# A streaming encoder layer on one core: all transposes of a PSUM bank issued before their reads, reads on two engines, norm and weight steps spaced anew, and down-projection loads one feature tile further on

## The chip, the cores and the metric

One Trainium2 chip, and one of its cores. The metric is the device time of one execution in microseconds; lower is better. The instructions of the core run on TensorE (PE in the profile, its weight loads PEld), VectorE (DVE), ScalarE (ACT), GpSimd (POOL) and SyncE (SP). In this kernel every DMA is issued by SP, in one queue.

## The reference

One layer of a streaming encoder for 1024 prompt positions and 8 samples of 16 positions (1152 rows of 1024 features, float32), both with the same weights. Cut to what matters here:

```python
def run_layer(x, c, ...):
    sh1, sc1, gt1, sh2, sc2, gt2 = ada_params(c, w_ada, b_ada)
    h = modulate(rms_norm(x, norm1_g), sh1, sc1)
    q, k, v, ub, vb, g_a, g_b = mixer_inputs(h, w_in, ...)
    ...                                   # band attention o_a, spatial gating o_b
    mixed = (g_a * (o_a @ w_out_a) + g_b * (o_b @ w_out_b)) @ w_out
    x = x + gt1 * mixed
    h2 = modulate(rms_norm(x, norm2_g), sh2, sc2)      # h * (1 + scale) + shift
    f, conv_state = conv_ffn(h2, conv_cache, ...)
    x = x + gt2 * f
    ...

def conv_ffn(h, conv_cache, w_ffn_in, ffn_conv_w, ffn_conv_b, w_ffn_out):
    g, u = jnp.split(h @ w_ffn_in, 2, axis=-1)         # 2816 features each
    gp = jnp.concatenate([conv_cache, g], axis=1)
    gc = ffn_conv_b
    for j in range(3):
        gc = gc + ffn_conv_w[j] * gp[:, j:j + T]
    return (jax.nn.gelu(gc) * u) @ w_ffn_out, gp[:, -2:]
```

## The kernel before, in words

The rows are nine tiles of 128 (tiles 0 to 7 the prompt, tile 8, called `NTP`, the samples). Every float32 product is done as three passes over a high and a low part: `split` (L76) copies the high part on ACT and subtracts on DVE for the low part. `load_w` (L80) is a DMA into a staging tile (`wst`, five buffers) and a split into a weight tile (`wp`, nine buffers).

The change lies in the second half of the kernel, which has three parts.

**Output projection and norm (L1124 to L1169).** Three passes: half 0 of the columns for tiles 8, 0, 1, 2, 3; half 1 for all nine; half 0 for 4 to 7. A tile and a half of the columns are eight steps k, and one step is three matmuls (`mxps`, L1140). After the eight steps DVE multiplies by the gate (L1153) and the old rows are added (L1154; on POOL in passes 0 and 1, on DVE in pass 2). When both halves of a tile are there, SP stores it (L1159), ACT squares it (L1116), POOL makes the factor (L125, L126), and DVE scales the tile in place (L1111). `later` holds these steps with the step number at which they enter the queues. The weights of the next pass are split during the last tile of a pass, one per step. PE, ACT and DVE run here in the order in which the program is written (`by_hand`, L1080); SP and POOL are ordered by the scheduler.

`between` writes, between the steps, the work for the first half of the feed-forward's rows: it transposes the scaled rows on PE into a bank of PSUM (`h2ps`, two banks), and `modulated` (L917) reads them with scale and shift into SBUF. Its items carry a tile, a flag and costs for ACT and DVE; `fill_in` emits one when the tile is far enough and both `credit` counters are above zero. `block_pair_1` does the same for the second half of the rows: eight items for tiles 3, 4, 5 (L999 to L1002), tile 6, two splits (`A11`, `A12`), tile 7, then sums and splits. For tiles 6 and 7 it writes one transpose, then its read, then the next transpose into the same bank, four times for each bank.

**Up-projection (L1354 to L1373).** 22 feature tiles f, two units u each (the halves of the rows). A unit is seven products X, Y, Z of 12 matmuls (L1199) with seven weight combinations B11, B21, T2, T1, T3, T4, B22 (`up_weights`, L1040), then the convolution, the GELU and a store to `aT_d`. The order by hand goes on until f = 0 is done, and the remaining items of `block_pair_1` are written into f = 0. Before f = 0 the convolution cache is loaded (`ccr`, L1184) and transposed (`ccps`, L1187). From f = 1 on, the scheduler orders all engines.

**Down-projection (`down_steps`, L1304).** Three groups of three row tiles; each goes over the 22 feature tiles, with three `load_w` for each f (`a`, `wfo_0`, `wfo_1`) and 18 matmuls (`fops`, L1320). The steps of f = 0 of the first group are written into the last feature tile of the up-projection. After it stand `conv_rows` (PE transposes, a DVE copy and five stores) and the loads of the last gate (`gate_rows`, 18 DMAs). At the end of a group, f = 20 and 21 are done accumulator by accumulator, and each is multiplied, added to the rows and stored (L1349 to L1351).

Of the kernel before, what the change touches and what calls it, by code (L numbers as in the profile page):

```python
# [12 lines left out]
ALU = mybir.AluOpType  # L13
AX = mybir.AxisListType

P = 128
D = 1024
KD = D // P
# [20 lines left out]
def tile_layer(ctx: ExitStack, tc: tile.TileContext, io):  # L39
# [30 lines left out]
    def tpps(name, n=512):  # L70
        return banks["pool"].tile([P, 512], F32, tag="tp", name=name, bufs=banks["tp"])[:, :n]
# [110 lines left out]
    r = 0  # L182
# [770 lines left out]

    ORDER = [NTP] + list(range(NTP))

    def between():


        o = opnd[0]
        yield 1, True, 0.65, 0.7  # L960
        o.raws(RAWS[:2])
        for h in range(2):
            ps = tpps(f"h2psS_{h}")
            for i in range(4):
                pe.transpose(ps[:, i * P:(i + 1) * P], x1[NTP][:, (4 * h + i) * P:(4 * h + i + 1) * P], ident)
            o.modulated_samples(RAWS[h], h, ps, 0)
            yield 1, True, 0.0, 1.4
        for k in range(KD):
            o.modulated(RAWS[k // 4], k, x1_T((0, 1), k, "0")[:, 0:QB - P], P)
            yield 1, True, 0.45, 0.0  # L970
        o.raws(RAWS[2:])
        yield 2, False, 1.3, 1.4
        o.chunks(0, ("A11h", "A11l", "A12h", "A12l", "A22h"))
        for n in ("A11", "A12"):
            o.split(n, HOME[n])
            yield 3, True, 1.3, 1.4
        for k in range(KD):
            o.modulated(RAWS[2 + k // 4], k, x1_T((1, 2, 3), k, "1")[:, 32:32 + QB], 0)
            yield 3, True, 0.65, 0.0
        o.raws(["S1"])  # L980
        for n in ("S1", "S3", "S2", "S4"):
            sums(o, (n,))
            yield 3, True, 0.0, 1.4
        for n in ("S2", "S1"):
            o.slots((n + "h", n + "l"))
            o.split(n, HOME[n])
            yield 3, True, 1.3, 1.4
        yield 5, False, 1.3, 1.4
        o.chunks(1, ("S3h", "S3l", "A22l", "S4h", "S4l"))
        for n in ("S3", "A22", "S4"):  # L990
            o.split(n, HOME[n])
            yield 5, False, 1.3, 1.4

    def block_pair_1():

        o = opnd[1]
        o.raws(RAWS)
        for k in range(KD):
            ps = x1_T((3, 4, 5), k, "2")  # L999
            o.modulated(RAWS[k // 4], k, ps[:, 64:64 + QB], 0)  # L1000
            o.modulated(RAWS[2 + k // 4], k, ps[:, 64 + QB:], 0)
            yield  # L1002
        for t in (6, 7):
            if t == 7:
                for n in ("A11", "A12"):
                    o.slots((n + "h", n + "l"))
                    o.split(n, HOME[n])
                    yield
            for h in range(2):
                ps = tpps(f"h2ps{t}_{h}")  # L1010
                for i in range(4):
                    pe.transpose(ps[:, i * P:(i + 1) * P], x1[t][:, (4 * h + i) * P:(4 * h + i + 1) * P], ident)
                    o.modulated(RAWS[2 + h], 4 * h + i, ps[:, i * P:(i + 1) * P], 32 + P * (t - 6))
            yield
        o.raws(["S1"])
        sums(o, ("S1", "S3", "S2"))
        o.chunks(2, ("A22h", "A22l", "S1h", "S3h", "S2h"))
        low_slot(o, "S2")
        yield
        sums(o, ("S4",))  # L1020
        low_slot(o, "S1")
        yield
        low_slot(o, "S3")
        yield
        o.split("A22", "22")
        yield
        o.slots(["S4h"])
        low_slot(o, "S4")
        yield
# [78 lines left out]

    def scale_tile(t, ss):
        r = rstd_of(ss, 1, D, nrm, f"x1n{t}r")  # L1110
        later.append((step_n + 3, lambda: dve.tensor_scalar(x1[t], x1[t], r, None, ALU.mult)))  # L1111
        scaled_at[t] = step_n + 5

    def square_tile(t):
        ss = nrm.tile([P, 1], F32, tag="ss", name=f"x1n{t}ss", bufs=4)
# [13 lines left out]
    for i, (blk, tiles) in enumerate(passes):  # L1129
        for t in tiles:  # L1130
# [6 lines left out]
            for k in range(KD):  # L1137
                w = wos[i][k]
                for n, (a, b) in enumerate(((hi, 0), (hi, 1), (lo, 0))):
                    pe.matmul(ps, lhsT=a[:, k, o:o + P], rhs=w[:, b, :], start=(k == n == 0), stop=(k == KD - 1 and n == 2))  # L1140
                step_n += 1
                for e in credit:
                    credit[e] = min(credit[e] + 0.72, 2.0)
                if t == tiles[-1] and next(loads[i + 1], loads) is not loads:
                    spend(0.63, 0.69)
                do_later()
                item = fill_in(item)
                if i == 2 and t == tiles[-1]:
# [5 lines left out]
            (pool if i < 2 else dve).tensor_tensor(x1[t][:, bs], x1[t][:, bs], xr, ALU.add)  # L1154
            spend(0.0, 0.7 if i < 2 else 1.4)
# [148 lines left out]
    def down_steps():  # L1304
        for g in range(3):
# [14 lines left out]
                    pe.matmul(acc[t, hf], lhsT=a[:, x, o], rhs=w[hf][:, y, :], start=(f == 0 and i == 0), stop=(f == NF - 1 and i == 2))  # L1320

            weights(0)
            for f in range(NF - 2):
                if f:
                    weights(f)
                for t in ts:
                    for hf in range(2):
                        step(f, t, hf)
                        if g == 0 and f == 0:
                            yield  # L1330
                if g == 0 and f == 0:
                    conv_rows()
                    g2p, g2s = stile(D, "g2p"), stile(D, "g2s")
                    for j in range(2):
# [1 line left out]

            for f in (NF - 2, NF - 1):
                weights(f)
            for t in ts:
                xr = stile(D, f"x1r{t}")  # L1340
                sp.dma_start(xr, x1_d[t * P:(t + 1) * P, :])
                y = stile(D, f"y{t}")
                gt = g2p if t < NTP else g2s
                dst = io["o_yp"].rearrange("b s d -> (b s) d")[t * P:(t + 1) * P, :] if t < NTP else io["o_ys"].rearrange("b s d -> (b s) d")
                for hf in range(2):
                    for f in (NF - 2, NF - 1):
                        step(f, t, hf)
                    hs = slice(512 * hf, 512 * (hf + 1))
                    dve.tensor_tensor(y[:, hs], acc[t, hf], gt[:, hs], ALU.mult)  # L1349
                    dve.tensor_tensor(y[:, hs], y[:, hs], xr[:, hs], ALU.add)  # L1350
                    sp.dma_start(dst[:, hs], y[:, hs])  # L1351
# [54 lines left out]
```

## Time and profile before

| | us |
|---|---|
| median of 3 runs | 1714.07 (1711.29 to 1717.16) |
| the profiled execution | 1715.13 |
| its span | 1713.3 |
| PE busy | 1654.2 |
| DVE busy | 917.8 |
| ACT busy | 731.4 |
| POOL busy | 338.2 |

PE is busy for 97% of the span. The page cuts the span into 40 slices of 42.8 us; each digit is the busy share in tenths, and a row of its own gives the TensorE clock that was granted. A matmul that runs at a lower clock counts as busy all the same, so both rows have to be read together.

### The profile page before, as it was taken

How to read it: one execution, taken by the hardware profiler on the slowest of the kernel's cores; microseconds unless marked ns; L12 is line 12 of the kernel's file. 1: busy time of each engine (PE TensorE's matmuls, PEld its weight loads, DVE VectorE, ACT ScalarE, POOL GpSimd, SP SyncE). 2: the span in 40 equal slices, each digit the busy share in tenths (PEclk: the TensorE clock that was granted, in tenths of full speed). 3: DMA queues.
4: the chain of work that ended last, by engine and by line, in shares of the span. 5: the costliest groups of instructions: out<-in, count | busy, mean ns of one | idle time of the engine just before them, and what ended most of it. 6: DMA issues, size and time to landing. Idle time of an engine off the chain costs nothing.

```text
span 1713.3 us, 28803 instructions
## 1 busy us (share of the span) xinstructions
PE 1654.2 (97%) x10788; PEld 1502.1 (88%) x10788; DVE 917.8 (54%) x1972; ACT 731.4 (43%) x1592; POOL 338.2 (20%) x506
## 2 busy tenths in 40 slices
PE   6999999999999999999887899999999998999998
PEld 5798888799998989998775899999999997888887
DVE  4552111137657543464365777776777664455554
ACT  5442111135655544552346444544444543334342
POOL 5410000024224200043222222222222210000000
PEclk9999999999999999999997999999999999999999
DMA  9125434421100132384321222222222224566664
GB/s 356 60 71 164 153 132 138 164 69 34 51 27 23 38 111 99 105 265 137 128 92 54 83 78 77 69 74 74 70 68 74 78 82 151 180 227 199 215 213 163
DMA packets 165552, 198.88 MB, mean 116 GB/s; under 512 B 14120, under 2 KB 124180, under 8 KB 165413
## 3 DMA queue, kind: packets, MB, share of 16 engines
q1 hardware_dynamic: 165413, 197.04, 35.8%
q8 instruction: 85, 1.39, 0.3%
q14 instruction: 54, 0.44, 0.1%
HBM read 161.48 MB, written 37.57 MB: 116 GB/s over the span
## 4 chain that ended last, share of the span: by engine, by line
PE 82%; DVE 5%; DMA 3%; ACT 3%; issue 3%; POOL 1%; SPq 1%; DVEq 0%; ACTq 0%; POOLq 0%
PE X L1199 15%; PE fops L1320 15%; PE Z L1199 8%; PE Y L1199 4%; PE o L688 2%; PE gbps L103 2%; PE qkps L101 2%; PE gbps L101 2%; PE gbps L102 2%; PE qkps L103 2%; PE qkps L102 2%; PE gaps L101 2%; PE gaps L102 2%; PE gaps L103 2%; PE adaps L382 2%
## 5 line engine op out<-in xcount | busy, mean ns | idle before, releaser
L1320 PE MATMUL fops<-wfo,a 128*128 128x512 f32 x1188 | 273.5, 392 | 6.6 <-ACT wfo L77 6.3
L1320 PEld LDWEIGHTS fops<-wfo,a 128*128 128x128 f32 x1188 | 224.5, 189 | 54.0 <-ACT wfo L77 6.7
L1199 PE MATMUL X<-op,wT 128*128 128x288 f32 x1144 | 194.8, 297 | 1.4 <-ACT u L1267 1.3
L1199 PEld LDWEIGHTS X<-op,wT 128*128 128x128 f32 x1144 | 169.1, 190 | 2.4 <-ACT u L1267 2.3
L1140 PE MATMUL mxps<-wo,mT 128*128 128x512 f32 x432 | 105.4, 399 | 2.9 <-ACT wo L77 1.8
L1140 PEld LDWEIGHTS mxps<-wo,mT 128*128 128x128 f32 x432 | 80.7, 191 | 20.4 <-ACT wo L77 2.5
L1232 DVE SCALAR_TENSOR_TENSOR gc<-gp,parT,gc 128x288 f32<-128x288 f32 (+2 forms) x110 | 67.6, 630 | 44.8 <-ACT gc L1231 44.8
L101 PE MATMUL qkps<-wqk,h1T 128*128 128x256 f32 x288 | 83.5, 290 | 0.8 <-ACT qf L582 0.8
L102 PE MATMUL qkps<-wqk,h1T 128*128 128x256 f32 x288 | 81.9, 284 | 0.0
L103 PE MATMUL qkps<-wqk,h1T 128*128 128x256 f32 x288 | 81.8, 284 | 0.0
L1231 ACT ACTIVATE gc<-gp,parT 128x288 f32<-128x288 f32 (+2 forms) x110 | 58.8, 572 | 39.1 <-DVE gp L1218 29.1
L1234 ACT ACTIVATE gc<-gc 128x288 f32<-128x288 f32 x88 | 39.0, 443 | 72.0 <-DVE gc L1233 72.0
L1059 POOL TENSOR_TENSOR t<-b,b 128x512 f32<-128x512 f32 x22 | 29.2, 1328 | 195.5 <-DVE wB L78 161.3
L101 PE MATMUL gaps<-h1T,wga 128*128 128x384 f32 x192 | 66.6, 347 | 0.0
L103 PE MATMUL gbps<-h1T,wgb 128*128 128x384 f32 x192 | 65.9, 343 | 0.0
L102 PE MATMUL gaps<-h1T,wga 128*128 128x384 f32 x192 | 65.0, 339 | 0.0
L101 PE MATMUL gbps<-h1T,wgb 128*128 128x384 f32 x192 | 64.9, 338 | 0.0
L102 PE MATMUL gbps<-h1T,wgb 128*128 128x384 f32 x192 | 64.7, 337 | 0.0
L78 DVE TENSOR_TENSOR wB<-b,wB 128x512 fp32r<-128x512 f32 x66 | 57.1, 867 | 13.5 <-ACT wB L77 12.2
L103 PE MATMUL gaps<-h1T,wga 128*128 128x384 f32 x192 | 64.2, 338 | 0.0
L1269 DVE TENSOR_TENSOR upb<-Z,u 128x288 f32<-128x288 f32 x44 | 20.0, 454 | 79.5 <-ACT u L1267 79.5
L78 DVE TENSOR_TENSOR wfo<-wfo_0s,wfo 128x512 fp32r<-128x512 f32 x66 | 45.7, 693 | 24.8 <-ACT wfo L77 24.6
(488 smaller groups left out, 4423.1 us busy)
## 6 DMA issues: line engine op xcount, KB each, us to landing
adaw<-in_w_ada_dram SPq DMA_DIRECT2D x48, 512.0 KB, 5.3
b<-in_w_ffn_in_dram SPq DMA_DIRECT2D x88, 256.0 KB, 4.0
wfo_0s<-in_w_ffn_out_dram SPq DMA_DIRECT2D x66, 256.0 KB, 3.0
wfo_1s<-in_w_ffn_out_dram SPq DMA_DIRECT2D x66, 256.0 KB, 2.6
aT_d<-gc SPq DMA_DIRECT2D x88, 144.0 KB, 2.8
mb_d<-sgb SPq DMA_DIRECT2D x8, 576.0 KB, 3.4
ga_d<-ga SPq DMA_DIRECT2D x24, 192.0 KB, 1.8
sga<-ga_d SPq DMA_DIRECT2D x8, 576.0 KB, 4.9
```

Source lines behind the costliest of these rows:

```text
L78: (eng or dve).tensor_tensor(lo, src, hi.bitcast(F32), ALU.subtract)
L101: pe.matmul(ps, lhsT=ah, rhs=bh, start=(i == 0), stop=False)
L102: pe.matmul(ps, lhsT=ah, rhs=bl, start=False, stop=False)
L103: pe.matmul(ps, lhsT=al, rhs=bh, start=False, stop=(i == n - 1))
L382: pe.matmul(ps[32 * j:32 * j + 32, :], lhsT=cT[:, k, :], rhs=st[j // 2][:, (j % 2) * 512:(j % 2 + 1) * 512], start=(k == 0), stop=(k == KD ...
L688: pe.matmul(o[hs, :], lhsT=v[:, k0 // P + i, hs], rhs=out[t, x][:, i * P:(i + 1) * P], start=(i == 0), stop=(i == nk - 1))
L1140: pe.matmul(ps, lhsT=a[:, k, o:o + P], rhs=w[:, b, :], start=(k == n == 0), stop=(k == KD - 1 and n == 2))
L1199: pe.matmul(ps, lhsT=w[:, wj, ks], rhs=x, start=(begin and n == 0), stop=(n == 11), skip_group_check=True)
L1231: act.activation(g, a0, AF.Identity, bias=bb, scale=w0)
L1232: dve.scalar_tensor_tensor(g, a1, w1, g, ALU.mult, ALU.add)
L1234: act.activation(gc, gc, AF.Gelu_apprx_tanh)
L1320: pe.matmul(acc[t, hf], lhsT=a[:, x, o], rhs=w[hf][:, y, :], start=(f == 0 and i == 0), stop=(f == NF - 1 and i == 2))
```

## The change

- A helper `transposed(t, h)` writes the four transposes of a bank and returns the bank. Tile 8 uses it (same order as before); for tiles 6 and 7 the four transposes of a bank now stand ahead of their four reads, and the reads go to ACT and DVE in turn.
- For tiles 3, 4, 5 the two reads of a bank go to ACT for even k and to DVE for odd k (all on ACT before).
- In `block_pair_1` the split of A11 follows tile 6, and that of A12 follows tile 7.
- A tile's square enters 3 steps after its store (2 before), the scaling 4 steps after the factor (3 before), and its transposes may follow 7 steps after the factor (5 before).
- The weights of the next pass begin one step earlier (the last step of the tile before the last). In pass 2 only four of the seven weight combinations of f = 0 are split; the other three (T3, T4, B22) are split in the first three steps of f = 0. `between` emits nothing in the last tile of pass 1.
- The old rows are added on POOL in pass 0 alone, on DVE in passes 1 and 2.
- After the passes no item of `block_pair_1` is written any more; tile 6 follows the first product of f = 0, the scaling of tile 7 stands after the second product's convolution, and tile 7's transposes follow the third product.
- `down_steps` asks for the loads of f + 1 ahead of the steps of f; `conv_rows` and the gate loads stand after f = 3 (f = 0 before). PE's order at the end of each group is fixed as written, and the last half row of the last tile is multiplied, added and stored in two halves.

```diff
+    def transposed(t, h):
+        ps = tpps(f"h2psT{t}_{h}")
+        for i in range(4):
+            pe.transpose(ps[:, i * P:(i + 1) * P], x1[t][:, (4 * h + i) * P:(4 * h + i + 1) * P], ident)
+        return ps
...
-            o.modulated(RAWS[k // 4], k, ps[:, 64:64 + QB], 0)
-            o.modulated(RAWS[2 + k // 4], k, ps[:, 64 + QB:], 0)
+            o.modulated(RAWS[k // 4], k, ps[:, 64:64 + QB], 0, k % 2 == 0)
+            o.modulated(RAWS[2 + k // 4], k, ps[:, 64 + QB:], 0, k % 2 == 0)
             yield
-        for t in (6, 7):
+        for t, n in ((6, "A11"), (7, "A12")):
+            for h in range(2):
+                ps = transposed(t, h)
+                for i in range(4):
+                    o.modulated(RAWS[2 + h], 4 * h + i, ps[:, i * P:(i + 1) * P], 32 + P * (t - 6), i % 2 == 0)
             if t == 7:
-                for n in ("A11", "A12"):
-                    o.slots((n + "h", n + "l"))
-                    o.split(n, HOME[n])
-                    yield
-            for h in range(2):
-                ps = tpps(f"h2ps{t}_{h}")
-                for i in range(4):
-                    pe.transpose(ps[:, i * P:(i + 1) * P], x1[t][:, ...], ident)
-                    o.modulated(RAWS[2 + h], 4 * h + i, ps[:, i * P:(i + 1) * P], 32 + P * (t - 6))
+                yield
+            o.slots((n + "h", n + "l"))
+            o.split(n, HOME[n])
             yield
...
-        later.append((step_n + 3, lambda: dve.tensor_scalar(x1[t], x1[t], r, None, ALU.mult)))
-        scaled_at[t] = step_n + 5
+        later.append((step_n + 4, lambda: dve.tensor_scalar(x1[t], x1[t], r, None, ALU.mult)))
+        scaled_at[t] = step_n + 7
...
-                if t == tiles[-1] and next(loads[i + 1], loads) is not loads:
-                    spend(0.63, 0.69)
+                last = t == tiles[-1]
+                if (last and (i < 2 or k in (1, 3, 5))) or (t == tiles[-2] and k == KD - 1):
+                    if next(loads[i + 1], loads) is not loads:
+                        spend(0.63, 0.69)
                 do_later()
-                item = fill_in(item)
+                if i != 1 or not last:
+                    item = fill_in(item)
...
-            (pool if i < 2 else dve).tensor_tensor(x1[t][:, bs], x1[t][:, bs], xr, ALU.add)
+            (pool if i == 0 else dve).tensor_tensor(x1[t][:, bs], x1[t][:, bs], xr, ALU.add)
...
-                later.append((step_n + 2, lambda t=t: square_tile(t)))
-    for _ in ws[0]:
-        pass
-    n = 0
-    while later or n < 3:
+                later.append((step_n + 3, lambda t=t: square_tile(t)))
+    while len(later) != 1 or later[0][0] - step_n > 4 or len(scaled_at) < NT:
         step_n += 1
         do_later()
-        if n < 3:
-            next(pair1)
-            n += 1
...
             weights(0)
+            weights(1)
             for f in range(NF - 2):
-                if f:
-                    weights(f)
+                if f and f < NF - 3:
+                    weights(f + 1)
...
-                if g == 0 and f == 0:
+                if g == 0 and f == 3:
                     conv_rows()
...
+            with tc.manual_schedule(engines={pe.engine}):      # around the end of a group
...
+                        n = 2 if t == ORDER[-1] and hf == 1 else 1
+                        for i in range(n):
+                            ...                                # multiply, add and store 512 / n columns
...
-                if f == 0 and (u, i) >= (0, 2):
-                    next(pair1, None)
+                if f == 0:
+                    if (u, i) == (0, 1):
+                        later.pop()[1]()
+                    else:
+                        next(pair1, None)
+                    next(ws[0], None)
```

More of the change, by code (lines that the diff above doesn't have):

```diff
@@ L962, in between @@
         for h in range(2):
-            ps = tpps(f"h2psS_{h}")
-            for i in range(4):
-                pe.transpose(ps[:, i * P:(i + 1) * P], x1[NTP][:, (4 * h + i) * P:(4 * h + i + 1) * P], ident)
-            o.modulated_samples(RAWS[h], h, ps, 0)
+            o.modulated_samples(RAWS[h], h, transposed(NTP, h), 0)
             yield 1, True, 0.0, 1.4
@@ L999, in block_pair_1 @@
             ps = x1_T((3, 4, 5), k, "2")
-            o.modulated(RAWS[k // 4], k, ps[:, 64:64 + QB], 0)
-            o.modulated(RAWS[2 + k // 4], k, ps[:, 64 + QB:], 0)
+            o.modulated(RAWS[k // 4], k, ps[:, 64:64 + QB], 0, k % 2 == 0)
+            o.modulated(RAWS[2 + k // 4], k, ps[:, 64 + QB:], 0, k % 2 == 0)
             yield
-        for t in (6, 7):
-            if t == 7:
-                for n in ("A11", "A12"):
-                    o.slots((n + "h", n + "l"))
-                    o.split(n, HOME[n])
-                    yield
-            for h in range(2):
-                ps = tpps(f"h2ps{t}_{h}")
-                for i in range(4):
-                    pe.transpose(ps[:, i * P:(i + 1) * P], x1[t][:, (4 * h + i) * P:(4 * h + i + 1) * P], ident)
-                    o.modulated(RAWS[2 + h], 4 * h + i, ps[:, i * P:(i + 1) * P], 32 + P * (t - 6))
+        for t, n in ((6, "A11"), (7, "A12")):
[3 more added lines that the diff above has]
+                    o.modulated(RAWS[2 + h], 4 * h + i, ps[:, i * P:(i + 1) * P], 32 + P * (t - 6), i % 2 == 0)
+            if t == 7:
+                yield
+            o.slots((n + "h", n + "l"))
+            o.split(n, HOME[n])
             yield
@@ L1143, in tile_layer @@
                     credit[e] = min(credit[e] + 0.72, 2.0)
-                if t == tiles[-1] and next(loads[i + 1], loads) is not loads:
-                    spend(0.63, 0.69)
+                last = t == tiles[-1]
+                if (last and (i < 2 or k in (1, 3, 5))) or (t == tiles[-2] and k == KD - 1):
+                    if next(loads[i + 1], loads) is not loads:
+                        spend(0.63, 0.69)
                 do_later()
-                item = fill_in(item)
-                if i == 2 and t == tiles[-1]:
+                if i != 1 or not last:
+                    item = fill_in(item)
+                if i == 2 and last:
                     for _ in fill:
@@ L1153, in tile_layer @@
             dve.tensor_tensor(x1[t][:, bs], ps, gt[:, bs], ALU.mult)
-            (pool if i < 2 else dve).tensor_tensor(x1[t][:, bs], x1[t][:, bs], xr, ALU.add)
-            spend(0.0, 0.7 if i < 2 else 1.4)
+            (pool if i == 0 else dve).tensor_tensor(x1[t][:, bs], x1[t][:, bs], xr, ALU.add)
+            spend(0.0, 0.7 if i == 0 else 1.4)
             halves_done[t] += 1
@@ L1338, in down_steps @@
                 weights(f)
[L1339 to L1351, printed above, removed]
+            with tc.manual_schedule(engines={pe.engine}):
+                for t in ts:
+                    xr = stile(D, f"x1r{t}")
+                    sp.dma_start(xr, x1_d[t * P:(t + 1) * P, :])
+                    y = stile(D, f"y{t}")
+                    gt = g2p if t < NTP else g2s
+                    dst = io["o_yp"].rearrange("b s d -> (b s) d")[t * P:(t + 1) * P, :] if t < NTP else io["o_ys"].rearrange("b s d -> (b s) d")
+                    for hf in range(2):
+                        for f in (NF - 2, NF - 1):
+                            step(f, t, hf)
+                        n = 2 if t == ORDER[-1] and hf == 1 else 1
+                        for i in range(n):
+                            hs = slice(512 * hf + i * 512 // n, 512 * hf + (i + 1) * 512 // n)
+                            dve.tensor_tensor(y[:, hs], acc[t, hf][:, i * 512 // n:(i + 1) * 512 // n], gt[:, hs], ALU.mult)
+                            dve.tensor_tensor(y[:, hs], y[:, hs], xr[:, hs], ALU.add)
+                            sp.dma_start(dst[:, hs], y[:, hs])
     prev = None
```

## The prediction

> **What bounds the kernel now.** I read the page first, then the busy times by stage, then the waits of PE, then the queues around each gap.
>
> ```profile
> span 1713.3 us, 28803 instructions
> PE   6999999999999999999887899999999998999998
> PEclk9999999999999999999997999999999999999999
> ```
>
> PE bounds: only four places of the span show less than full PE. The first slice isn't touched. The others are the end of the output projection with the first feature tile (slices 20 to 23), the start of the down-projection (slice 34) and the last slice. Cut at the edges of those stages (columns: wall; PE, PEld, DVE, ACT, POOL busy; granted clock; DMA share; GB/s):
>
> ```profile
> 833.96:863.32 29.36, 24.49 (x119) 19.52 (x117) 9.27 (x12) 11.91 (x21) 5.48 (x8) 0.88 0.21 75
> 863.32:896.16 32.84, 29.93 (x130) 23.45 (x129) 23.77 (x27) 13.44 (x21) 9.77 (x9) 1.00 0.34 113
> 896.16:907.04 10.88, 9.00 (x46) 5.77 (x44) 7.98 (x13) 9.13 (x22) 4.24 (x5) 1.00 0.25 86
> 907.04:914.94 7.90, 3.53 (x11) 1.87 (x12) 1.94 (x4) 4.65 (x12) 0.00 (x0) 0.65 0.51 169
> 914.94:964.64 49.70, 39.75 (x239) 37.80 (x238) 32.22 (x46) 25.83 (x47) 9.69 (x12) 0.82 0.14 38
> 1003.12:1025.50 22.38, 22.38 (x171) 22.38 (x170) 15.90 (x31) 10.85 (x24) 6.21 (x8) 1.00 0.25 74
> 1433.50:1450.00 16.50, 10.20 (x34) 8.22 (x34) 7.95 (x14) 6.56 (x11) 0.00 (x0) 0.79 0.71 224
> ```
>
> The row from 1003.12 is one feature tile in the steady state: 14 products in 22.38 us, 1.6 us each, PE never idle. What a step and a transpose cost when nothing waits:
>
> ```profile
> 784.92 49.20 PE L1140 MATMUL mxps<-wo,mT 128*128 128x512 f32 x216
> 833.96 1.03 PE L965 MATMUL h2psS<-ident,x 128*128 128x128 f32 x8
> 834.75 2.30 PE L1140 MATMUL mxps<-wo,mT 128*128 128x512 f32 x9
> ```
>
> 72 steps in 49.04 us are 0.68 us a step (216 matmuls); eight transposes take 0.79, about 0.09 each. So what the stages lose, by their work:
> - 833.96 to 863.32: 23 steps (15.65) and 48 transposes (4.1) in 29.36: lost 9.6.
> - to 896.16: 42 steps (28.6) in 32.84: lost 4.2.
> - to 907.04: 7 steps (4.8) and 24 transposes (2.0) in 10.88: lost 4.1.
> - to 914.94: tile 6's eight transposes and three for `ccps` (1.1) in 7.90: lost 6.8.
> - to 964.64: 19 products (30.4) and tile 7's transposes (0.8) in 49.70: lost 18.5, the low clock (0.82) included.
> - 1433.50 to 1450: 6.3 us of wait, and 10.2 us at 0.79 of the clock, 2.1 more: lost 8.4.
>
> All that is 51.6 us; no change in these places can bring more.
>
> **The change part by part.**
>
> *Spacing of norm steps, and adds on DVE in pass 1.*
>
> ```profile
> x_d<-x SPq DMA_DIRECT2D x9, 512.0 KB, 2.9
> 829.33 0.75 DVE L1111 TENSOR_SCALAR x<-x,x1n0r 128x1024 f32<-128x1024 f32 x1 [4.38 <-DMA x_d<-x]
> 840.45 1.06 ACT L1116 ACTIVATE junk<-x 128x1024 f32<-128x1024 f32 x1 [7.21 <-POOL x L1154]
> 842.02 1.11 PE L935 MATMUL h2ps<-ident,x 128*128 128x128 f32 x4 [3.15 <-ACT raw L921]
> ```
>
> The scaling stands at the head of DVE's queue for 4.38 us until the tile's store has landed, and the next tile's multiply is behind it. Then ACT stands at the square until POOL has added, the reads of the bank are behind that square, and PE waits 3.15 for a bank. With the scaling at the end of a tile's eight steps, the store (2.9 us to landing) is over when DVE gets there; the add on DVE follows the multiply at once. It costs DVE nine times about 0.7 us, in a stage where DVE is busy 9.27 of 29.36; without that cover it would be 0.7 per tile of 5.45. What is late next: eight short transposes for tiles 0 and 1 go at the pace of ACT's reads. I keep 1.5 of the 9.6: gain 8.1. Bounds: nothing, if the store lands late again; 9.6.
>
> *Weights of the next pass one step earlier, two splits moved out of their way.* PE's waits for the late halves of `wo` go; I keep 0.5 of the 4.2: gain 3.7 (0 to 4.2). In SP's queue the loads stand where they stood, as slots come free; POOL has lost nine adds and delays nobody.
>
> *Tiles 3, 4, 5 on two engines, four weight splits in pass 2 for seven.* ACT did 16 reads, seven weight copies and a square among 24 transposes. Each bank now has one reader, so DVE takes eight reads without a meeting. But the scaling of tile 5 still enters after the split of S4 and B11, and the first transposes wait for it, about 1.2; the DVE reads stand behind split T2, about 0.9 more. I keep 2.2 of 4.1: gain 1.9 (-1 to 4.1).
>
> *Tile 6.*
>
> ```profile
> 909.23 0.46 ACT L921 ACTIVATE raw<-h2ps,S,G 128x128 f32<-128x128 f32 x1 [0.42 <-PE h2ps L1012]
> 910.25 0.46 ACT L921 ACTIVATE raw<-h2ps,S,G 128x128 f32<-128x128 f32 x1 [0.56 <-PE h2ps L1012]
> PE h2ps L1012 <- ACT raw L921: 10.8, 13, 3.5
> ```
>
> A transpose waits for the read of its neighbour in the bank and the read for the transpose: 1.02 us a pair, 16 pairs. Four transposes together end that. With tile 6 behind the first product, PE has no wait there. In its place comes `ccps`, now the last thing ahead of the first product:
>
> ```profile
> L1184 SPq DMA_DIRECT2D ccr<-in_cache_ffn_conv_dram x3: 333/380/423, 903.5 to 904.4; - x3
> DMA to landing us min/median/max: 1.7/1.7/1.7
> ```
>
> Its staging tile is that of combination T1, which is now split at step six of the last tile: three issues and 1.7 us of flight later PE has been through for some 1.3 us. Gain 6.8 - 1.3 = 5.5 (3 to 6.8).
>
> *Feature tile 0.* This is where I am least sure. Tile 7's transposes follow the third product, and its scaling follows on DVE the reads of tile 6, the A11 split, the T3 split and the second product's convolution. How two engines share a bank shows here, in the attention stage:
>
> ```profile
> 374.68 0.28 DVE L579 TENSOR_TENSOR kk<-qkt,kk 64x128 fp32r<-64x128 f32 x1
> 374.99 0.27 ACT L578 ACTIVATE kk<-qkt 64x128 fp32r<-64x128 f32 x1 [0.64 <-DVE kk L579]
> 375.30 0.29 DVE L579 TENSOR_TENSOR kk<-qkt,kk 64x128 fp32r<-64x128 f32 x1 [0.34 <-ACT kk L578]
> ACT qf L582 <- DVE kk L579: 13.9, 19, 1.4
> PE X L1199 <- ACT u L1267: 1.3, 1, 1.3
> ```
>
> `qf` needs nothing that DVE writes, and still waits: reads of one bank go one after the other, one hop for each. So tile 6's eight reads make a chain of seven hops (four of 0.5 on ACT, three of some 0.35 on DVE), about 3.1 us, where ACT alone would take about as long, and two engines free of each other 2.0 (four reads of 0.5 on each).
>
> [...]
>
> ```profile
> 916.09 1.15 ACT L914 ACTIVATE opA11h<-raw 128x1152 fp32r<-128x1152 f32 x1
> 919.57 1.35 DVE L915 TENSOR_TENSOR opA12l<-raw,opA12h 128x1152 fp32r<-128x1152 f32 x1
> 938.30 0.69 DVE L78 TENSOR_TENSOR wB<-b,wB 128x512 fp32r<-128x512 f32 x1
> 921.97 0.51 DVE L1255 TENSOR_TENSOR gp<-Y,x1c 128x160 f32<-128x160 f32 x2
> 924.03 0.35 DVE L1233 SCALAR_TENSOR_TENSOR gc<-gp,parT,gc 128x128 f32<-128x128 f32 x1
> ```
>
> From the end of the first product: reads 3.1, high part 1.15, low part 1.35, T3's low part 0.69, sums and convolution 2.4 (921.97 to 924.38), scaling 0.75: 9.4. PE has tile 6's transposes and two products in that time, 4.0. So PE waits 5.4 for tile 7, in place of one of 3.5 and several shorter ones before; and a wait of that size brings the clock down as before 1450, 2.1. Further on DVE is the late one: it was busy 32.22 in this stretch, and takes over eight reads (2.8), three splits (2.1) and the A11 split (1.35), some 38 us, against 31.2 of PE work. Not all is needed in the stretch, and f = 1 leaves DVE 6.5 us free (15.90 of 22.38). I take 16 of loss for the 18.5 plus 1.3 that follows it (PE's wait for `u`): between 12, with the waits of tile 7, S2 and S1 alone, and 20, as now. Gain 3.8 (0 to 8).
>
> *Down-projection.*
>
> ```profile
> 1405.74 8.57 SPq L828 DMA_DIRECT2D g2s<-ada_d  x16
> 1426.04 0.40 SPq L93 DMA_DIRECT2D a_1s<-aT_d  x1
> 1435.28 1.30 SPq L1301 DMA_DIRECT2D o_cs_dram<-glo  x3
> 1436.67 0.34 SPq L93 DMA_DIRECT2D wfo_0s<-in_w_ffn_out_dram  x1
> PE fops L1320 <- ACT wfo L77: 6.3, 1, 6.3
> ```
>
> SP has the weights of f = 1 behind the stores of `conv_rows`, which wait for the last unit. Asked for ahead of f = 0, they pass them and the 18 gate loads; a weight tile for each comes free by the fourth-last product. PE then has 4.1 us of work for each feature tile (18 matmuls at 0.68 for three) while three loads come. The 18 gate loads, 8.57 us of SP, are asked for later; they were issued 10 us ahead of their place in the program, so I expect them in a gap of SP again, and if they fall among the weights of f = 3 to 5 they cost up to 8.6 less the lead. I keep 1.2 of 8.4: gain 7.2 (0 to 8.4).
>
> *End.* The last chain is two DVE passes and a store:
>
> ```profile
> 1709.18 1.28 DVE L1350 TENSOR_TENSOR y<-y,x1r 128x512 f32<-128x512 f32 x2
> o_yp_dram<-y SPq DMA_DIRECT2D x16, 256.0 KB, 3.2
> aT_d<-gc SPq DMA_DIRECT2D x88, 144.0 KB, 2.8
> ```
>
> After PE's end (1708.55) DVE works until 1710.46. In halves, and with the other accumulator done before, it ends about 0.4 sooner, and half the bytes land some 0.4 sooner: gain 0.8 (-0.5 to 1.5). PE's fixed order costs nothing, since five of six accumulators are read before the sixth ends.
>
> **The sum.** 8.1 + 3.7 + 1.9 + 5.5 + 3.8 + 7.2 + 0.8 = 31.0. The profiled execution took 1715.13 (span 1713.3), 1.06 above the median; against the median, 1714.07 - 31.0 = 1683.1, so 1683.
>
> **The rivals.**
> - *Feature tile 0 takes it back.* DVE or ACT, in fixed order, has one late item after the other, and the loss there grows from 19.8 to about 28: 12 us less gain, 1695. For it: DVE's 38 us against 31.2. Against: 17 us of DVE's 49.7 were idle.
> - *Better than that.* Both readers of a bank run at once and f = 1's products fill the waits: 16 becomes 9, and 5 of the 6.7 that I kept elsewhere go: 1671. Against: the `qf` row.
> - *The weights of f = 1 stay late*, behind another store in SP's queue: 7.2 less, 1690.
> - *Slower.* The down-projection asks one tile further while the ring of nine weight tiles holds three. If a split then falls on PE's path in each of some 63 feature tiles, it costs 63 times the excess; from 0.5 us each (4.1 becomes 4.6) it outweighs all the rest, and at 0.7 the time is 1727. Against: the slots are freed by the same matmuls as before.
> - *No change*: the waits only move into feature tile 0 and the loads' order changes nothing: 1714.
>
> **How the numbers follow.** Forecast 0.5, feature tile 0 takes it back 0.17, better 0.12, late weights 0.1, slower 0.06, no change 0.05. A run can tell 0.3%, 5.1 us. So faster 0.89, same 0.05, slower 0.06. The forecast's own range is 1675 to 1691; with the better case and the two partial ones, 1669 to 1705 leaves out 2 in 10 or less.
>
> **What would show it.** Right: the pairs of L1012 are gone, PE passes 863 with no wait above 1 us, the first product starts near 894 (914.94 before), one wait of about 5 us ahead of tile 7's transposes, PE's wait for `wfo` under 1.5 us. Wrong: waits of PE in feature tile 0 that sum to over 20 us, a feature tile of the down-projection above 4.1 us, or the gate loads in one block among the weights.

## The result, and the profile after

| | median, us | runs | ratio to before, 95% |
|---|---|---|---|
| before | 1714.79 | 4 (1711.29 to 1717.16) | |
| changed kernel | 1691.24 | 4 (1688.30 to 1692.72) | 0.9862 (0.9839 to 0.9885) |

The change saves 23.6 us. The profiled execution took 1688.30 us, the lowest of its four, with a span of 1686.4, so the two profiles differ by more, 26.9. The head of the page after, to be held against the same three rows of before:

```profile
span 1686.4 us, 28806 instructions
PE   5999999999999999999996999999999999999998
PEclk9999999999999999999998999999999999999999
```

Of the four thin places, three are left: the two ends, and the stretch around the first feature tile, now in slice 22 (counted from 1, as in the prediction), with a 6 in PE and an 8 in the clock. The start of the down-projection is a 9 now. By stage (wall; PE, PEld, DVE, ACT, POOL busy; granted clock; DMA share; GB/s):

```profile
783.13:856.89 73.76, 73.13 (x344) 59.66 (x343) 31.49 (x45) 22.38 (x39) 12.91 (x17) 1.00 0.42 136
856.89:884.13 27.24, 27.02 (x120) 21.92 (x119) 20.44 (x25) 11.52 (x18) 5.20 (x6) 1.00 0.42 133
884.13:897.87 13.74, 9.54 (x46) 7.16 (x45) 10.53 (x18) 8.23 (x17) 4.24 (x6) 0.88 0.17 63
898.12:956.03 57.91, 45.00 (x295) 43.50 (x293) 43.41 (x71) 30.20 (x57) 14.89 (x17) 0.85 0.21 63
1417.47:1436.00 18.53, 18.53 (x86) 15.32 (x85) 12.62 (x23) 9.86 (x18) 0.00 (x0) 1.00 0.70 221
```

The first two rows, passes 1 and 2 up to the last tile, are full and at clock 1.00: that gain is real. The last row, the start of the down-projection, is full too. The third and the fourth row, the last tile and feature tile 0, are not: 13.74 us for 6.8 us of work, and 57.91 us of which PE was busy for 45.00 at a clock of 0.85. (The fourth row holds feature tile 0 and some nine products of feature tile 1; below, "feature tile 0" as a stage means such a stretch.) What PE waits for there, in the chain of waits (total, times, longest):

```profile
PE h2psT L960 <- DVE x L1113: 4.7, 1, 4.7
PE X L1198 <- ACT x1c L1246: 4.2, 1, 4.2
PE h2ps L935 <- DVE x L1113: 3.7, 1, 3.7
PE h2psT L960 <- DVE ccT L1187: 1.7, 1, 1.7
PE Z L1198 <- ACT op L914: 1.2, 1, 1.2
```

The 3.7 is in the last tile; it was not there before. It is the scaling of tile 5. DVE's queue around it (start, duration, idle time before):

```profile
873.09 1.35 DVE L915 TENSOR_TENSOR opS2l<-raw,opS2h 128x1152 fp32r<-128x1152 f32 x1
874.36 1.35 DVE L915 TENSOR_TENSOR opS1l<-rawS,opS1h 128x1152 fp32r<-128x1152 f32 x1
875.63 0.68 DVE L1158 TENSOR_TENSOR x<-mxps,g1p 128x512 f32<-128x512 f32 x1
...
880.17 0.76 DVE L1113 TENSOR_SCALAR x<-x,x1n4r 128x1024 f32<-128x1024 f32 x1 [2.76 <-DMA x_d<-x]
...
884.12 2.76 DVE L915 TENSOR_TENSOR op<-raw,op 128x576 fp32r<-128x576 f32 x4 [0.61 <-ACT op L914]
886.80 0.68 DVE L78 TENSOR_TENSOR wB<-b,wB 128x512 fp32r<-128x512 f32 x1
887.41 0.75 DVE L1113 TENSOR_SCALAR x<-x,x1n5r 128x1024 f32<-128x1024 f32 x1
```

Read from the bottom: the scaling of tile 5 (887.41) stands behind the low parts of S3, A22, S4 and B11, these behind the scaling of tile 4 (880.17), which stood 2.76 us for that tile's store; the store was late because tile 4's multiply (875.63) stood behind the low parts of S2 and S1. Before the change those two splits were written in tile 6 of pass 1. What moved them follows from the order that the program writes: by the new spacing the transposes of tiles 1, 2 and 3 enter three steps later, the four sums behind them end only in the sixth step of tile 6, which leaves no credit in that tile, the last tile of the pass takes no items, and S2 and S1 come in the third and fifth step of pass 2. The adds that went to DVE are charged to the credit that lets items into the queue (1.4 a tile instead of 0.7), but that does not decide it: with 0.7 the two would stand in the first and third step of pass 2, and with 1.4 and the old spacing in the fifth and seventh step of tile 6 of pass 1. No run varies the spacing alone.

### The profile page after: what moved, and what is told of

Read it like the earlier page. It is cut to its first block, busy times and chain, and to the rows that moved or that the text cites. A ratio compares the mean times of both kernels' runs of the same rounds, so it can differ in the third digit from the quotient of the medians.

```text
span 1686.4 us, 28806 instructions
## 1 busy us (share of the span) xinstructions
PE 1639.1 (97%) x10788; PEld 1493.7 (89%) x10788; DVE 922.3 (55%) x1999; ACT 723.6 (43%) x1576; POOL 327.0 (19%) x497
## 4 chain that ended last, share of the span: by engine, by line
PE 90%; DVE 4%; DMA 2%; ACT 2%; issue 1%; POOL 0%; SPq 0%; DVEq 0%; ACTq 0%; POOLq 0%
PE fops L1319 16%; PE X L1198 16%; PE Z L1198 8%; PE mxps L1142 4%; PE Y L1198 4%; PE o L688 2%; PE gbps L103 2%; PE qkps L101 2%; PE gbps L101 2%; PE gbps L102 2%; PE qkps L103 2%; PE qkps L102 2%; PE gaps L101 2%; PE gaps L102 2%; PE gaps L103 2%; PE adaps L382 2%
## 5 line engine op out<-in xcount | busy, mean ns | idle before, releaser
L609 ACT ACTIVATE sc<-sc,st 128x640 f32<-128x640 f32 (+4 forms) x64 | 44.5, 695 | 31.0 <-DVE st L608 30.6
```

Source lines behind the costliest of these rows:

```text
L609: act.activation(s, s, AF.Exp, bias=m, accum_out=ssum)
```

## Experiments

Each comparison below is made by stage, for a reason that the profiles gave: the output projection begins at 784.92 in the profile of before, and between 781.95 and 788.79 in the thirteen others, though the code up to there is the same in all. The start is read from the first step of the output projection, the "first product" is that of feature tile 0.

**Halves: the down-projection alone (e1), all but it (e2).** Edits: `down_steps` of after in the kernel before, and the reverse.

> The kernel before with the new down-projection alone (loads asked for one feature tile ahead, the rows of the convolution and the last gate's loads after f = 3, fixed order on PE at the end of a group, last half row in two halves). Theory A (what the two traces say by their offsets: 16.5 us between the ends of the up-projection, 26.6 between PE's ends): about 10 us less than before, some 1704 to 1705, with no wait of PE at the first products. Theory B (the prediction's price, 7.2 and 0.8 at the end): 8 us less, 1707. Theory C (part of what the offsets show is luck of the profiled pair): under 5 us.

> The changed kernel with the down-projection of before, so the other half of the change alone. If the two halves add (they lie 450 us apart, nothing couples them): 16 to 17 us less than before by theory A of e1, that is about 1698, and 10 us more than the changed kernel; by theory B 18 to 19 less, 1696. If it comes out below 10 us less, the halves do not add and the first half has cost something in the second.

e1: 1703.88 us, ratio 0.9943 (0.9927 to 0.9959). e2: 1703.17, 0.9934 (0.9921 to 0.9946). From the four profiles:

| | output start to first product | first product to end of span |
|---|---|---|
| before | 130.02 | 798.36 |
| after | 114.99 | 788.28 |
| e1 | 129.74 | 788.38 |
| e2 | 114.51 | 798.91 |

The halves do not touch each other: each row takes its first number from one parent and its second from the other, within 0.6. The down-projection is worth 10.0 to 10.6 us by the traces (10.3 by the medians), more than the 7.2 and 0.8 forecast: theory A. The other half is worth 14.8 to 15.5 ahead of the first product and nothing after it. e2's median shows only 11.1 for it; its profiled run, of the median's time, began the output projection 3.0 us later than before did. Why the first 785 us vary like that was not settled. In kernels with the new down-projection 24 of its matmuls stand ahead of the last product of the up-projection, 12 before, so the time from first to last product below can be compared only between kernels with the same down-projection.

**Grouped transposes alone (e3).** In the kernel before, for tiles 6 and 7:

```diff
                 for i in range(4):
                     pe.transpose(ps[:, i * P:(i + 1) * P], x1[t][:, ...], ident)
+                for i in range(4):
                     o.modulated(RAWS[2 + h], 4 * h + i, ps[:, i * P:(i + 1) * P], 32 + P * (t - 6))
```

> The kernel before with one edit: for tiles 6 and 7 the four transposes of a bank stand ahead of their four reads, all reads on ACT. Sixteen pairs at 1.02 us become four groups of 0.4 for transposes and 4 reads of about 0.45, two banks in turn: about 4 us less per tile. Theory A (pairs were what PE waited for, at both tiles): 7 to 8 us less, 1707. Theory B (head of line: at tile 6 the wait goes, at tile 7 DVE's or ACT's next late item takes its place): 3 to 4 us less, 1711. Rival (a moved wait only): within 1.5 us of before.

1708.91, ratio 0.9971 (0.9961 to 0.9981), by which it is 5.0 us less. PE's waits from 890 to 975:

```profile
PE X L1200 <- ACT u L1268: 9.7, 2, 5.6
PE Z L1200 <- ACT wT L77: 1.8, 1, 1.8
...
PE h2ps L1012 <- ACT raw L921: 0.7, 1, 0.7
```

The pairs' 10.8 us are down to 0.7, and 9.7 stand in a new place, ahead of a product. The first product comes 5.4 us earlier (124.61 us after the start), and the way from there to the last product of the up-projection is as long as before (516.82; 516.45). Tile 6's part was real, tile 7's turned into another wait: theory B, with a larger tile 6.

**One engine for each bank (e4).**

```diff
-  o.modulated(RAWS[2 + h], ..., 32 + P * (t - 6), i % 2 == 0)
+  o.modulated(RAWS[2 + h], ..., 32 + P * (t - 6), h == 0)
```

> The changed kernel; for tiles 6 and 7 the first bank's four reads go to ACT and the second bank's four to DVE, instead of turn and turn about in each bank. Theory A (the hops of 0.5 us are one bank's, the two engines exclude each other there): reads of tile 7 take about 1.5 to 2.0 us from first to last instead of 3.1, no wait between ACT's and DVE's reads, and tile 7's transposes wait 0.7 to 1.1 less than 4.7; the time 1 to 2 us less than the changed kernel. Rival (the order of program, not the bank, makes the hops): 0.5 us hops stay and the time is the same within 0.5 us.

1689.73, ratio 0.9860 (0.9845 to 0.9876): not to be told from the changed kernel. The reads of tile 7 in the changed kernel, ACT's and DVE's (start, duration, idle before):

```profile
911.77 0.46 ACT L921 ACTIVATE raw<-h2psT,S,G 128x128 f32<-128x128 f32 x1 [0.47 <-PE h2psT L960]
912.26 0.41 DVE L923 TENSOR_SCALAR raw<-h2psT,G,S 128x128 f32<-128x128 f32 x1 [0.53 <-ACT raw L921]
912.71 0.81 ACT L921 ACTIVATE raw<-h2psT,S,G 128x128 f32<-128x128 f32 x2 [0.48 <-DVE raw L923]
...
914.49 0.41 DVE L923 TENSOR_SCALAR raw<-h2psT,G,S 128x128 f32<-128x128 f32 x1 [0.53 <-ACT raw L921]
```

and in e4:

```profile
916.08 1.50 ACT L921 ACTIVATE raw<-h2psT,S,G 128x128 f32<-128x128 f32 x4 [0.47 <-PE h2psT L960]
916.93 1.37 DVE L923 TENSOR_SCALAR raw<-h2psT,G,S 128x128 f32<-128x128 f32 x4 [0.90 <-PE h2psT L960]
```

Above, each engine's idle time ends with the other's read: hop after hop, 3.13 us from first to last. Below, each engine's four reads run through, 2.22 us, and both engines are busy at once, each in its own bank, from 916.93 to 917.58. So sharing a bank makes the hops: theory A. In this edit each engine also gets its own destination tile `raw`; against that as the cause stands `qf` in the prediction, which hops (13.9 us in 19 waits) though DVE writes another tile. In all these rows one engine's read of a bank begins after the other's has ended (0.48 us idle on ACT, 0.53 on DVE, in the rows above); no run lets two engines into one bank at once, so what the chip would do then is not shown here. PE's wait ahead of tile 7's transposes fell to 3.54, and first to last product takes 518.01 us for 519.21; the run's time can't show 1 us.

**The place of tile 7's scaling (e5).**

```diff
-                    if (u, i) == (0, 1):
-                        later.pop()[1]()
-                    else:
-                        next(pair1, None)
+                    next(pair1, None)
+                    if (u, i) == (0, 0):
+                        later.pop()[1]()
```

with the split of A11 one item later.

> The changed kernel with the scaling of tile 7 right behind the reads of tile 6 on DVE, ahead of the T3 split, the convolution and the A11 split, which then stands behind the second product's convolution. Theory A (DVE's queue as a whole is the late one in feature tile 0: between 905.5 and 927.6 it was busy for about 18.3 of 22.1 us): the wait of 4.7 ahead of tile 7's transposes goes below 1, and the wait ahead of the third product of unit 1 grows from 4.2 to 7 or 8; feature tile 0 is 3 to 4 us shorter, the time about 1688. Theory B (the place of the scaling was the only fault): the 4.7 and the low clock behind it, about 2, are gained, the 4.2 stays; 1684 to 1685. Rival C (the second wait takes all): no change, 1691.

1691.41, ratio 0.9866 (0.9853 to 0.9880). PE's waits:

```profile
PE X L1197 <- ACT x1c L1245: 5.3, 1, 5.3
...
PE X L1197 <- ACT u L1259: 2.7, 1, 2.7
```

The 4.7 is gone, 2.7 and 1.1 more at `x1c` have come, and the 295 matmuls from the first product on take 57.76 us instead of 57.91. Rival C: the whole wait moved. A gave the right reason and a wrong size: it counted on DVE's idle time in that stretch being usable, and it was not, since DVE there waits again and again for ACT: for a high part before it can make the low part (1.73 us for A11's, 0.36 for A12's), and for ACT's reads in the shared bank (0.53 at a time).

**Less ahead of S2 (e8).**

```diff
-        sums(o, ("S1", "S3", "S2"))
+        o.sum("S1", "11", "21", ALU.subtract)       # S3
+        o.sum("11", "22", "S1", ALU.subtract)       # S2 = 22 - S3; S1 follows after S2's split
...
-                if u == 1 or i >= 3:
+                if u == 1 or (i >= 3 and f > 0):
                     next(nxt, None)
```

> The changed kernel with two pieces of DVE work taken out of the queue ahead of S2 of unit 1: S2 is formed from S3 (22 minus S3), so that the sum S1 (2.36 us there) comes after it, and the weights of feature tile 1 are split from unit 1 on only (B11's low part, 1.78, and its copy on ACT). Nothing is left out. Theory A (the 4.2 us wait at unit 1's third product is DVE's queue ahead of S2, not the copy x1c that the row names): that wait falls to 0.5 or less, and the low clock behind it (0.50 to 935) goes; feature tile 0 is 4 to 6 us shorter, if the work that was put off does not come late in unit 1: 1686. Theory B (it comes late in unit 1, since DVE's sum of work is what counts): waits ahead of S1 or of f = 1 take the place, 1 to 2 us gained, 1689 to 1690.

1691.92, ratio 0.9864 (0.9850 to 0.9878). PE's waits:

```profile
PE Z L1202 <- ACT op L914: 3.6, 1, 3.6
PE X L1202 <- ACT u L1270: 2.3, 1, 2.3
```

The 4.2 is gone, as both theories had it, so `x1c` was only the last name in that row: it stood on ACT behind S2's high part, ahead of which ACT was idle for 8.02 us in the changed kernel until DVE's sums were there. But the next product's operand (S1) and the weights that had been put off are late now. Theory B, with nothing gained at all: first to last product takes 521.11 us for 519.21.

**The same queue made longer and shorter (e11, e9).** Both on the kernel of e6 (below). e11 computes the low part of A11 twice, with the same values:

```diff
             o.split(n, HOME[n])
+            if n == "A11":
+                dve.tensor_tensor(o.g["A11l"][0], o.r["11"], o.g["A11h"][0].bitcast(F32), ALU.subtract)
```

> The kernel of e6 with the low part of A11 of unit 1 computed twice on DVE (1.36 us more there, same values, nothing else). Theory A (DVE's queue in its fixed order sets the length of feature tile 0): tile 7's scaling and everything behind it is 1.3 later, and the 295 matmuls from the first product on take 59.1 to 59.3 us instead of 57.8. Rival (DVE has slack there, idle for about 7 of the first 30 us): under 0.4 us more.

e9 gives all reads of tiles 3, 4 and 5 to ACT:

```diff
-            o.modulated(RAWS[k // 4], k, ps[:, 64:64 + QB], 0, k % 2 == 0)
+            o.modulated(RAWS[k // 4], k, ps[:, 64:64 + QB], 0)
```

> The kernel of e6, with all sixteen reads of tiles 3, 4 and 5 on ACT, as before the change. Theory A (DVE is the late engine in the last tile): DVE loses 3.2 us of reads, but ACT has 16 reads of 0.43, four weight copies of 0.63 and a square, 10.5 us in a stretch of 9.9; the last tile (9.9 us in e6) stays within 1 us of it, and the two readers were worth nothing much. Theory B (the prediction's: two readers are worth about 2 us there): the last tile is 2 us or more longer, with waits for ACT's reads, 1687. Both ends are far below the -1 to 4.1 of the prediction if it stays within 0.5.

e11: 1687.00, ratio 0.9843 (0.9828 to 0.9857). e9: 1685.27, 0.9829 (0.9816 to 0.9842). The stretch of 295 matmuls (e11: 296) from the first product on, in e6, e11 and e9 (columns as in the stages above; DVE is the third busy time):

```profile
894.42:952.25 57.83, 45.80 (x295) 44.35 (x293) 43.36 (x71) 30.20 (x57) 14.71 (x17) 0.85 0.22 65
```

```profile
894.90:954.17 59.27, 42.58 (x296) 41.17 (x294) 44.72 (x72) 30.12 (x57) 14.77 (x17) 0.91 0.22 63
```

```profile
895.60:952.32 56.72, 45.04 (x295) 43.55 (x293) 42.23 (x69) 30.63 (x59) 14.90 (x17) 0.85 0.22 67
```

DVE has 1.36 us more to do in e11, and the stretch is 1.44 longer; 1.13 less in e9 (two instructions fewer), and it is 1.11 shorter. The stretch less DVE's busy time is 14.47, 14.55 and 14.49 in the three, and 14.50 in the changed kernel, while PE's busy time follows neither. PE's wait for tile 7's scaling grows from 4.71 in e6 to 6.11 in e11. This is what "DVE's fixed order sets feature tile 0" looks like: theory A of e11. The rest of 14.5 belongs to this order, in which DVE also waits for ACT: where reads or sums stand otherwise it is 10.7 (e4), 8.6 (e10) and 12.4 (e12), so DVE's busy time alone gives the length only between kernels with the same order. In the last tile e9 took 10.66 us from its first transposes to the first product, e6 10.45: the two readers of tiles 3, 4 and 5 were worth 0.2, theory A of e9.

**The splits of S2 and S1 in DVE's idle time (e6).**

```diff
                 if i != 1 or not last:
                     item = fill_in(item)
+                elif k == 4:
+                    for _ in range(2):
+                        spend(1.3, 1.4)
+                        item = next(fill)
```

> The changed kernel with the splits of S2 and S1 written between the weights wo_5 and wo_6 in the last tile of pass 1, where ACT and DVE waited 2.7 and 2.3 us for the load of wo_6; in the changed kernel they stand at the third and fifth step of pass 2, ahead of tile 4's multiply. Theory A (the last tile is late because DVE's fixed order brings tile 4 late, and with it scale 4, tile 5 and scale 5): tile 4's multiply starts 2 to 2.7 us earlier, the wait of 3.7 for the scaling of tile 5 falls to about 1.5 to 2, and the stretch from the first output step to the first product is 1.5 to 2 us shorter. Rival B (the store's landing or the low parts of S3, A22 and S4 set that scaling): the wait stays at 3.7. Rival C (the weights wo_6 and wo_7 now come late): PE gets a new wait of about 1 us ahead of pass 2's steps and nothing is gained.

1685.25, ratio 0.9831 (0.9817 to 0.9844). DVE's queue, to be held against that of the result:

```profile
867.85 1.36 DVE L915 TENSOR_TENSOR opS2l<-raw,opS2h 128x1152 fp32r<-128x1152 f32 x1
...
870.39 0.69 DVE L78 TENSOR_TENSOR wo<-wo_6s,wo 128x512 fp32r<-128x512 f32 x1
...
872.92 0.68 DVE L1162 TENSOR_TENSOR x<-mxps,g1p 128x512 f32<-128x512 f32 x1
...
877.83 0.75 DVE L1113 TENSOR_SCALAR x<-x,x1n4r 128x1024 f32<-128x1024 f32 x1 [3.50 <-POOL x1n4r L126]
...
885.07 0.75 DVE L1113 TENSOR_SCALAR x<-x,x1n5r 128x1024 f32<-128x1024 f32 x1
```

and the last tile:

```profile
883.97:894.15 10.18, 8.24 (x47) 5.96 (x45) 8.27 (x15) 6.07 (x14) 4.41 (x5) 1.00 0.19 71
```

The two splits fit into the time in which DVE had waited for the load of `wo_6`, whose own split is no later for it. Tile 4's multiply starts 2.6 us earlier than in the changed kernel (counted from the output start), both scalings 2.3, PE's wait falls from 3.7 to 1.5, and since the clock stays at 1.00 instead of 0.88 the last tile is 3.6 us shorter, more than theory A gave. Output start to first product: 111.37 us (114.99).

**The scaling of tile 5 earlier (e7).**

```diff
-        later.append((step_n + 4, lambda: dve.tensor_scalar(...)))
+        later.append((step_n + (2 if t == 5 else 4), lambda: dve.tensor_scalar(...)))
```

> The changed kernel with the scaling of tile 5 two steps earlier on DVE, ahead of the low parts of S4 and the split of B11. Theory A (order alone): PE's wait for that scaling falls from 3.7 to about 1.7, and the stretch to the first product is 2 us shorter. Theory B (DVE is full from 880 to 891, so what is moved back comes late itself): the first transposes start 2 us earlier but a bank's read on DVE comes late in their place, and the stretch is shorter by less than 0.7.

1688.39, ratio 0.9856 (0.9843 to 0.9869). The edit passed only the low part of B11 (0.68), not S4's: the wait fell from 3.69 to 3.06, and output start to first product is 114.73, 0.26 less. That is theory B's size, but with so little moved it tells the theories apart only weakly.

**The parts that helped, together (e10, e12).** e10 is e6 with e4, e7 and the sums of e8 (not its weights); e12 is e10 with e9's reads.

> The kernel of e6 with e4's reads (one bank, one engine), e7's scaling of tile 5 two steps earlier, and S2 of unit 1 formed from S3 so that its sum S1 follows (the weights of feature tile 1 stay where they are, unlike in e8). If the parts keep what their own traces showed (1.2 in feature tile 0 from e4, 0.3 from e7, 1 to 2 from the sum): 2 to 3 us less than e6, about 1682.5. If what is late at the end of feature tile 0 is the chain of the weights of feature tile 2 (their load, POOL's sums, ACT's copy, then the copy of X behind it on ACT, a wait of 0.7 in the changed kernel and 1.6 in e4), that wait grows by what is gained ahead of it and the time is that of e6 within 1 us.

> The kernel of e10 with e9's reads of tiles 3, 4 and 5 (all on ACT). In the traces e9 lost 0.2 us in the last tile and won 1.1 in feature tile 0 against e6. If DVE's queue is still what sets feature tile 0, the stretch from the first product to the last of the up-projection (515.8 in e10) gets about 1 us shorter, and the time is 1683 (within 1 us of it), the best of all; if e10 has used that gain up already, it is e10's 1684 within 1 us.

e10: 1683.93, ratio 0.9822 (0.9808 to 0.9835). From the first to the last product of the up-projection it takes 515.84 us (e6: 519.13), and the wait of `X` for `u` at the end of feature tile 0, blamed on the weights of feature tile 2, is gone instead of longer: that explanation falls. PE's wait for S1's operand has grown to 4.40. By the medians e10 is only 1.3 us under e6; in the profiled pair its output projection began 2.5 us later. e12: 1682.40 (1679.30 to 1685.14), ratio 0.9817 (0.9802 to 0.9831), the lowest median of all, 8.8 us under the changed kernel, but not to be told from e10; the stretch is 515.54, so e10 had used up most of e9's gain.

## Why the prediction was right, step by step

Forecast 1683, measured 1691.24: the sign and the main causes held, 31.0 us of terms gave 23.6. The time lies 0.24 above the forecast's own range (1675 to 1691) and inside the wide one (1669 to 1705). Of the signs named beforehand, the pairs of L1012 are gone, no wait of PE up to 863 is above 0.4, PE never waits for `wfo`, and a feature tile of the down-projection takes 4.1 us (264.4 for 1164 matmuls). The first product came 114.99 us after the output start, where 894 meant 109.1. By the two profiled executions, whose difference is 26.9:

- *Spacing and adds in pass 1*: 8.1 forecast. The 73.76 us hold 98 steps and 48 transposes, 70.8 of work: lost 3.0 for 9.6, so 6.6. Right; the largest wait left is 0.36.
- *Weights of the next pass*: 3.7 forecast; 27.24 for 39 steps (26.5): lost 0.7 for 4.2, so 3.5. Right.
- *Last tile*: 1.9 of gain forecast, 2.8 worse measured (13.74 for 6.8 of work, so 6.9 lost for 4.1 before). Here a step failed. It had the scaling of tile 5 behind S4 and B11, 1.2 us, but took DVE's queue ahead of that from the trace of before, where S2 and S1 had been split in pass 1. What the new spacing did to that order was not followed. e6 puts the two back into DVE's idle time, and the stretch is down to 10.18 (10.88 before). The 2 us that two readers were to bring are 0.2 in e9.
- *Tile 6*: 5.5 forecast, 6.8 measured: the first product follows `ccps` at 898.12 with no wait. The 1.3 us at `ccps` did not come. Its copy to SBUF did hold up the second bank of tile 6 by 1.7, a wait that stands inside feature tile 0: on DVE that copy (L1187) stood 1.27 us for ACT's square of tile 7.
- *Feature tile 0*: 3.8 forecast. e2 gives it apart: first to last product of the up-projection 516.80, 0.35 more than before, with 0.8 of tile 6's transposes in it, so 0.45. The wait for tile 7 was forecast well (5.4; 4.71). The failed step is the one after it: the sum took 16 of loss, halfway between 12, "with the waits of tile 7, S2 and S1 alone", and 20, "as now", and so reckoned by PE's waits, as if taking one away shortened the rest. The loss was 19.3 (57.91 for 279 matmuls of products, 37.2, and 16 transposes, 1.4): PE stood idle for 12.9, and its matmuls took 6.4 longer, most of it at the low clock. In e11 PE is busy 3.2 less than in e6 and the stretch is still longer, so the clock is not what sets it. e5, e8 and e11 show that the order on DVE does, and the change left DVE more work there: 43.4 busy, 41.3 in as many matmuls before.
- *Down-projection and end*: 7.2 and 0.8 forecast, 10.0 in e1. The end gave 0.4: from PE's end to DVE's it is 1.46 for 1.92, as forecast, but from there to the end of the span 2.93 for 2.87, so the smaller store brought nothing. The loss at the start was undercounted: it was cut at 1433.50 and valued by the mean clock. A fair cut of before, against the last row of the stages after:

```profile
1431.52:1450.00 18.48, 12.18 (x45) 9.56 (x44) 9.93 (x18) 7.42 (x13) 0.00 (x0) 0.82 0.63 201
```

In the same wall time PE did 45 matmuls before and does 86 now; 41 at 0.227 (three to a step of 0.68) are 9.3 us.
- Some 1.8 us of the 26.9 lie ahead of the output projection, outside the change.

Without that last item the parts come to 24.6. Tile 6 and the down-projection brought 3.3 more than forecast, the last tile and feature tile 0 came out 8.0 short; that the time is no further off owes something to luck.

Of the rivals, "feature tile 0 takes it back" named the right engine and too high a price (12; it was 3.3 under the forecast). Its 1695 is nearer to the time than 1683 is, but more of what is missing comes from the last tile. The ring of nine weight tiles did no harm: PE has no wait from 960 on in the changed kernel, nor in the down-projection of e1. The sixteen loads of `g2s` were issued from 1389.26 to 1399.83, among the first weights, and held up nothing.

## What to carry to other kernels

Where an engine worked in a fixed order and was late, a wait of PE named only the last item in the queue: moving that item moved the wait (e3: 10.8 us down to 0.7, with 9.7 in a new place; e5: 4.7 gone, 2.7 and 1.1 more elsewhere; e8: 4.2 gone, waits of 3.6 and 2.3 elsewhere), and what helped was work taken off that engine or put where it sat idle (e9: 1.13 us less on DVE, the stretch 1.11 shorter; e6: the last tile 3.6 shorter). Doubling one harmless instruction on the suspected engine, and seeing whether the stage grows by just that (e11: 1.36 us more on DVE, 1.44 longer), tells in one run whether its queue sets the pace there. When a change moves steps of a hand-written order, follow the order it then produces; the queue of the old trace is no longer the queue.

## What the chip showed that was not expected

*The clock after a wait.* Granted clock (third column from the right) in the 3 to 4 us after a wait of 1.52 us (e6), 3.55 (e10), 3.54 (e12) and 4.71 (changed kernel):

```profile
885.87:889.00 3.13, 3.09 (x16) 2.25 (x16) 2.95 (x5) 2.75 (x6) 1.61 (x2) 1.00 0.22 90
```

```profile
908.30:912.00 3.70, 3.70 (x30) 3.70 (x31) 2.75 (x6) 3.70 (x9) 0.00 (x0) 1.00 0.26 71
```

```profile
906.17:910.00 3.83, 3.83 (x19) 3.83 (x20) 2.66 (x6) 3.63 (x9) 0.00 (x0) 0.55 0.24 68
```

```profile
910.65:915.00 4.35, 4.35 (x19) 4.35 (x20) 2.27 (x5) 2.92 (x8) 0.00 (x0) 0.50 0.22 60
```

The same wait of 3.5 us left the clock alone in e10 and halved it in e12: 30 matmuls against 19 in about the same time, and PE counts as busy throughout both (3.70 us of 3.70, 3.83 of 3.83). After a shorter wait, 2.66 us in e5, the clock was low too (0.62 from 915.03 to 919.50). What decides between them is not shown; what the traces do show is when the clock changed. Between 800 and 1480 us of the profiles of before and after, it was either 1.00 or 0.50, and its changes lie a multiple of 3.41 us apart: after the change it was 0.50 for 3.41 us from 887.87, 6.83 from 908.35 and 10.24 from 925.42. Cut by those changes into stretches of 3.41 us, the eight at full clock with 1.75 us or more free of matmuls were each followed by half the clock, and none of those with 1.55 or less was. An estimate for the other two, from the clocks of e12 (0.55 from 906.17 to 910.00) and e10 (0.63 from 922.03 to 928.00): it fell at about 906.5 and 923.6. The 3.41 us before the first hold 3.1 of e12's wait; counted back from the second in steps of 3.41, e10's wait falls into two parts of about 1.8, and neither was followed by half the clock. So near 1.8 it went both ways.

*DVE beside POOL.* In the changed kernel a low part of 1152 columns took 1.36 us (905.53) and one of 512 took 0.69 (911.04), both while POOL was idle. Beside POOL's sums, DVE's first and then POOL's rows:

```profile
916.06 2.23 DVE L915 TENSOR_TENSOR opA12l<-raw,opA12h 128x1152 fp32r<-128x1152 f32 x1 [0.36 <-ACT opA12h L914]
918.21 1.78 DVE L78 TENSOR_TENSOR wB<-b,wB 128x512 fp32r<-128x512 f32 x1
```

```profile
915.77 1.30 POOL L1061 TENSOR_TENSOR t<-b,b 128x512 f32<-128x512 f32 x1 [13.26 <-DVE wB L78]
917.15 2.29 POOL L1062 TENSOR_TENSOR b<-b,b 128x512 f32<-128x512 f32 x1
```

Each DVE row is longer by 0.9 and 1.1, about what was left of POOL's instruction when it began (1.0 and 1.2). The rows show these lengths; what makes DVE take longer they do not show. If it is POOL's sums, they cost DVE 2.0 us here, in a stage that DVE's queue sets; no run moved them away.
